# Norm tails of the GLU and the output projection: sums and products by column parts, and Newton steps on GpSimd

## The chip, the cores and the metric

The kernel runs on one core of a Trainium2 chip. The metric is the device time of one execution in microseconds (us), smaller is better. Five engines have queues of their own, each worked off in order: TensorE (PE; its weight loads are listed as PEld), VectorE (DVE), ScalarE (ACT), GpSimd (POOL) and SyncE (SP), which here issues most DMAs. Matmul results lie in PSUM, everything else on the chip in SBUF.

## What is computed

One inference step of a decoder trunk of two layers, for a prompt of 1024 tokens and 64 sample tokens (8 sequences of 8), model width D = 1024, in float32. Of the reference, the two places that matter here:

```python
def rmsnorm(x, g):
    y = xf * lax.rsqrt(jnp.mean(xf * xf, axis=-1, keepdims=True) + NORM_EPS)
    return (y * g)

def s5_mixer(...):                     # layer 0; ends with a gated linear unit (GLU)
    ...
    gl = z @ w_glu
    out = gl[..., :D_MODEL] * jax.nn.sigmoid(gl[..., D_MODEL:])

def trunk(...):
    # layer 0
    x = x + rmsnorm(a_out, p['a_post_g'][i])                 # a_out of s5_mixer
    # layer 1
    x = x + rmsnorm(o @ p['w_o'][j], p['b_post_g'][j])       # o of the attention
    # in both layers then
    f_out, buf = conv_ffn(rmsnorm(x, p['f_pre_g'][i]), ...)
    x = x + rmsnorm(f_out, p['f_post_g'][i])
```

Between the GLU or the output projection and the next feed-forward stage (conv_ffn, an up projection, a short convolution and a down projection) each token row therefore goes through two norms: the post-norm of what was just projected, and, after the residual is added, the pre-norm of the feed-forward stage.

## The kernel before

The tokens lie in nine tiles: eight of 128 prompt tokens (0 to 7) and one of the 64 sample tokens (8). A product in float32 is made of three matmuls over parts of high and low precision (`mm3`, L800 to L802), so operands are split into `hi` and `lo` (`split_evac`: a cast on ScalarE, L136, and a difference on VectorE, L137).

The **GLU** (`glu`) goes over the output columns in four passes `q` of 256 columns, and in each pass over the tiles in the order 0, 3, 1, 4, 2, 5, 6, 8, 7. Per tile and pass TensorE makes the two halves of `gl` in PSUM, ScalarE the sigmoid (L1022), VectorE the gated product into `ao[tt]` (L1023). In the last pass (q = 3) the row of a tile is complete, and its tail begins.

The **output projection** (`o_proj`) takes the tiles in the order 8, 0, 3, 1, 4, 2, 5, 6, 7. Columns 0 to 511 were made earlier and are loaded from `yod`; columns 512 to 1023 are made here, and copied out of PSUM by ScalarE (L1960). The tail follows per tile.

The **tail** of a tile has three parts. `tail_a`: the square sum of the row on ScalarE (L815), the product with the post-norm gain on VectorE (L829), the reciprocal root `r` of the mean square (`rstd_from`), and `r*y + xr` with the residual `xr` (L832), which is also stored. `tail_n`: the square sum of the result (L815 again), a second `rstd_from`, and the product with `r` and the pre-norm gain (L842). `tail_b`, some tiles later (`tail.lag`): TensorE transposes the row (L848) and `split_evac` splits it into the operand of the up projection. Tiles 3 to 5 also take part in pairs (`Combos.pair`: tile 0 with 3, 1 with 4, 2 with 5), where VectorE first makes four differences (L889 to L892).

`rstd_from` computes on 128x1 operands: L118 scales the sum, L119 makes a first guess from the bit pattern, and three Newton rounds follow, each L122 and L126, all on VectorE and each dependent on the one before it. A tile needs this twice.

The order of the instructions on each engine is not the order of the code: a scheduler places them by its own timing model, and so a change of one part shifts the neighbours too. Where the work of two tiles is ready, their Newton rounds are interleaved.

Of the kernel before, what the change touches and what calls it, by code (L numbers as in the profile page):

```python
# [10 lines left out]
F32 = mybir.dt.float32  # L11
# [62 lines left out]
def trunk_kernel(ctx, tc, I, O):  # L74
# [33 lines left out]
    def flat(t, n=512):  # L108
        return t[:, 0:n]

    def rstd_from(pool, ss, n, parts, tag, n_mean=D, bufs=None):

        kw = {"bufs": bufs} if bufs else {}
        v = pool.tile([P, n], F32, tag=tag + "v", name=nm("rv"), **kw)
        s = pool.tile([P, n], F32, tag=tag + "s", name=nm("rs"), **kw)
        r = pool.tile([P, n], F32, tag=tag + "r", name=nm("rr"), **kw)
        p = slice(0, parts)
        V.tensor_scalar(v[p], ss, -0.5 / n_mean, -0.5 * EPS, op0=ALU.mult, op1=ALU.add)  # L118
        V.tensor_scalar(r[p].bitcast(I32), v[p].bitcast(I32), -0.5, RSQ_MAGIC, op0=ALU.mult, op1=ALU.add)  # L119
        for _ in range(3):  # L120
            if n == 1:
                V.scalar_tensor_tensor(s[p], r[p], r[p], v[p], op0=ALU.mult, op1=ALU.mult)  # L122
            else:
                V.tensor_tensor(s[p], r[p], r[p], ALU.mult)
                V.tensor_tensor(s[p], s[p], v[p], ALU.mult)
            V.scalar_tensor_tensor(r[p], s[p], 1.5, r[p], op0=ALU.add, op1=ALU.mult)  # L126
        return r
# [684 lines left out]
    def square_sum(y, n):  # L812
        junk = slot("junk", dtype=BF16)
        ss = slot("ss")
        A.activation(junk[0:n], y, AF.Square, accum_out=ss[0:n])  # L815
        return ss[0:n]

    def rms_rstd(t, n):
        return rstd_from(pools["ph"], square_sum(t, n), 1, n, "n1", bufs=4)

    def tail_a(y, tt, post, xsrc, xdst, last=False):

        t0, n = tokens(tt)
        xr = slot("xr")
        nc.sync.dma_start(xr[0:n], xsrc(tt))
        halves = (slice(512, D), slice(0, 512)) if last else (slice(0, D),)
        ss = square_sum(y, n)
        for hs in halves:
            V.tensor_tensor(y[:, hs], y[:, hs], post[0:n, hs], ALU.mult)  # L829
        r = rstd_from(pools["ph"], ss, 1, n, "n1", bufs=4)  # L830
        for hs in halves:
            V.scalar_tensor_tensor(y[:, hs], y[:, hs], r[0:n], xr[0:n, hs], op0=ALU.mult, op1=ALU.add)  # L832
            nc.sync.dma_start(xdst(tt)[:, hs], y[:, hs])

    def tail_n(y, tt, gain=None):

        n = tokens(tt)[1]
        r = rms_rstd(y, n)
        if gain is None:
            A.mul(y, y, r[0:n])  # L840
        else:
            V.scalar_tensor_tensor(y, y, r[0:n], gain[0:n], op0=ALU.mult, op1=ALU.mult)  # L842
# [55 lines left out]
    class Tail:  # L898
# [2 lines left out]

        def __init__(self):
            self.n, self.q, self.combos, self.gain, self.lag = [], [], None, None, 2

        def add(self, y, tt, *a):
            tail_a(y, tt, *a)
# [86 lines left out]
    def glu(ws):  # L993
# [10 lines left out]
        for q in range(4):  # L1004
            if q:
                ws = glu_units(q)
            qs_ = slice(q * 256, (q + 1) * 256)
            for tt in ORDER_U:
                n = tokens(tt)[1]
                if q == 0:  # L1010
                    ao[tt] = slot("acc")
                    if tt == ORDER_U[4]:
                        tail_b(zt, NTT)
                        xsx = sample_pair()
                ps = tok_mm(tt, ws, None if n == P else xsx)
                if n < P:
                    g = slot("gr")[0:n]
                    fold_sample(g, ps)
                else:
                    g = ps  # L1020
                sg = slot("gr")
                A.activation(sg[0:n, 0:256], g[:, 256:512], AF.Sigmoid)  # L1022
                V.tensor_tensor(ao[tt][0:n, qs_], g[:, 0:256], sg[0:n, 0:256], ALU.mult)  # L1023
                if q == 3:
                    if tt == 0:
                        tail.combos = Combos()
                    y = ao[tt][0:n, 0:D]
                    tail.add(y, tt, post, x_in, x_scr(x1d))
            if q == 0:
                conv_params(0)  # L1030
                lam_column(cpool)
# [307 lines left out]

    def ffn_down(dn, i, xsrc, xdst, norm):  # L1340
        acc = {}
        post = [None]
        nch = len(dn.plan)

# [600 lines left out]
    def o_proj():  # L1945

        ws = half_units(I["w_o"][0], 1)
        post = row_bcast(I["b_post_g"][0])
        tail.gain, tail.lag = row_bcast(I["f_pre_g"][1]), 1
        conv_params(1)  # L1950
        xsx = sample_pair()
        for tt in ORDER_O:
            if tt == 0:
                tail.combos = Combos()
            t0, n = tokens(tt)
            y = slot("acc")
            nc.sync.dma_start(y[0:n, 0:512], yod[t0 : t0 + n])
            ps = tok_mm(tt, ws, xsx)
            if n == P:
                A.copy(y[:, 512:D], ps)  # L1960
            else:
                fold_sample(y[0:n, 512:D], ps)
            tail.add(y[0:n, 0:D], tt, post, x_scr(x2d), x_scr(x3d))
# [67 lines left out]
```

## Time and profile before

| | us |
|---|---|
| median of three runs (lowest, highest) | 2731.77 (2730.25, 2734.73) |
| profiled execution: its time, its span | 2735.75, 2734.0 |
| busy of the span: PE, DVE, ACT, POOL | 2519.4, 1957.0, 1260.9, 694.3 |

The profiled execution is 4 us above the median. The span goes from the first to the last instruction of that execution. Busy shares over the whole span mix stages with different limits; the stages that the change touches last from about 240 us (start of the GLU) to 490 us, and from about 1880 us to 1980 us (the output projection and its tails). In the profile's rows a duration is that of one record; records of neighbouring instructions on one engine can overlap by their start-up. "<-" names what ended an engine's wait.

### The profile page before, as it was taken

How to read it: one execution, taken by the hardware profiler on the slowest of the kernel's cores; microseconds unless marked ns; L12 is line 12 of the kernel's file. 1: busy time of each engine (PE TensorE's matmuls, PEld its weight loads, DVE VectorE, ACT ScalarE, POOL GpSimd, SP SyncE). 2: the span in 40 equal slices, each digit the busy share in tenths (PEclk: the TensorE clock that was granted, in tenths of full speed). 3: DMA queues.
4: the chain of work that ended last, by engine and by line, in shares of the span. 5: the costliest groups of instructions: out<-in, count | busy, mean ns of one | idle time of the engine just before them, and what ended most of it. 6: DMA issues, size and time to landing. Idle time of an engine off the chain costs nothing.

```text
span 2734.0 us, 39538 instructions
## 1 busy us (share of the span) xinstructions
PE 2519.4 (92%) x14362; PEld 2208.4 (81%) x14362; DVE 1957.0 (72%) x3719; ACT 1260.9 (46%) x2475; POOL 694.3 (25%) x943
## 2 busy tenths in 40 slices
PE   5778997999999989999999899999699999998996
PEld 3767886999999967778776788887599999996774
DVE  6994339677776789985222688866877767779998
ACT  5762225444444454344322677753444444454332
POOL 3220000111322375501201322200021222337661
PEclk9999998999999999999999999999899999999998
DMA  4343213222222233345645333325322222233324
GB/s 131 96 105 87 84 62 101 64 73 72 73 72 73 87 122 95 108 132 177 214 156 200 101 77 91 99 89 157 103 70 75 73 72 73 72 108 100 102 86 146
DMA packets 257702, 278.63 MB, mean 102 GB/s; under 512 B 41772, under 2 KB 205924, under 8 KB 257508
## 3 DMA queue, kind: packets, MB, share of 16 engines
q1 hardware_dynamic: 253188, 263.85, 31.3%
q0 software_dynamic: 3232, 10.29, 1.7%
q8 instruction: 114, 1.87, 0.3%
q10 hardware_dynamic: 1088, 1.97, 0.2%
q14 instruction: 80, 0.66, 0.1%
HBM read 187.82 MB, written 68.58 MB: 94 GB/s over the span
## 4 chain that ended last, share of the span: by engine, by line
PE 38%; DVE 9%; DMA 3%; ACT 3%; issue 2%; POOL 1%; SPq 0%; DVEq 0%; POOLq 0%; ACTq 0%
PE mm L800 11%; PE mm L801 10%; PE mm L802 10%; DVE S L1846 1%; ACT S L1850 1%; PE mm L1373 1%; DVE acc L1384 1%; DVE S L1860 1%; PE mm L1874 1%; DMA gr<-gd 1%; PE tr L848 1%; DVE qx L1789 1%; DMA raw<-in_w_down_dram 1%; DMA raw<-in_w_v_dram 1%; POOL xr L1265 0%
## 5 line engine op out<-in xcount | busy, mean ns | idle before, releaser
L800 PE MATMUL mm<-xT_hi,whi 128*128 128x320 f32 (+1 forms) x1408 | 459.4, 328 | 6.6 <-ACT xT_hi L136 3.4
L801 PE MATMUL mm<-xT_lo,whi 128*128 128x320 f32 (+1 forms) x1408 | 456.3, 324 | 0.1
L802 PE MATMUL mm<-xT_hi,wlo 128*128 128x384 f32 (+1 forms) x1408 | 454.7, 324 | 0.0
L1162 POOL COPY cvo<-acc 128x2 f32<-128x2 f32 x88 | 157.5, 1789 | 677.6 <-ACT acc L1145 677.6
L800 PEld LDWEIGHTS mm<-xT_hi,whi 128*128 128x128 f32 x1408 | 265.2, 189 | 15.6 <-DVE acc L1128 9.6
L137 DVE TENSOR_TENSOR wlo<-raw,whi 128x1024 fp32r<-128x1024 f32 x88 | 107.5, 1222 | 233.8 <-PE mm L801 227.3
L801 PEld LDWEIGHTS mm<-xT_lo,whi 128*128 128x128 f32 x1408 | 266.0, 189 | 0.9 <-DVE xT_lo L137 0.9
L802 PEld LDWEIGHTS mm<-xT_hi,wlo 128*128 128x128 f32 x1408 | 265.7, 189 | 0.2
L1159 DVE SCALAR_TENSOR_TENSOR acc<-acc,cpar,acc 128x1104 f32<-128x1104 f32 x176 | 238.8, 1377 | 0.7 <-ACT acc L1157 0.5
L800 PE MATMUL mm<-whi,xT_hi 128*128 128x512 f32 x576 | 228.6, 401 | 4.2 <-ACT whi L783 4.2
L801 PE MATMUL mm<-wlo,xT_hi 128*128 128x512 f32 x576 | 228.1, 397 | 0.0
L802 PE MATMUL mm<-whi,xT_lo 128*128 128x512 f32 x576 | 227.4, 397 | 0.0
L136 ACT CAST whi<-raw 128x1024 fp32r<-128x1024 f32 x88 | 92.7, 1054 | 286.1 <-PE mm L802 261.3
L1384 DVE TENSOR_TENSOR acc<-mm,acc 128x512 f32<-128x512 f32 x279 | 183.7, 678 | 5.0 <-PE mm L802 4.5
L800 PE MATMUL mm<-acc,whi 128*128 128x384 f32 x528 | 179.8, 341 | 3.1 <-DVE acc L1119 2.8
L801 PE MATMUL mm<-acc,whi 128*128 128x384 f32 x528 | 179.9, 341 | 0.0
L802 PE MATMUL mm<-acc,wlo 128*128 128x384 f32 x528 | 179.7, 341 | 0.0
L800 PEld LDWEIGHTS mm<-whi,xT_hi 128*128 128x128 f32 x576 | 108.7, 189 | 33.5 <-ACT whi L783 4.4
L802 PEld LDWEIGHTS mm<-whi,xT_lo 128*128 128x128 f32 x576 | 108.2, 188 | 26.6 <-issue 0.9
L1157 ACT ACTIVATE acc<-acc,cpar 128x1104 f32<-128x1104 f32 x88 | 115.4, 1313 | 30.5 <-DVE acc L1128 19.9
L801 PEld LDWEIGHTS mm<-wlo,xT_hi 128*128 128x128 f32 x576 | 108.2, 188 | 25.8 <-issue 0.4
L1846 DVE CUSTOM_DVE_ANT_0 S<-mm,tb 128x512 f32<-128x512 f32 (+3 forms) x192 | 101.1, 551 | 27.5 <-PE mm L1844 24.2
(563 smaller groups left out, 6255.9 us busy)
## 6 DMA issues: line engine op xcount, KB each, us to landing
raw<-in_w_up_dram SPq DMA_DIRECT2D x88, 512.0 KB
gd<-acc SPq DMA_DIRECT2D x44, 552.0 KB
raw<-in_w_down_dram SPq DMA_DIRECT2D x44, 512.0 KB
gr<-gd SPq DMA_DIRECT2D x80, 256.0 KB
raw<-in_glu_w_dram SPq DMA_DIRECT2D x32, 256.0 KB
acc<-in_cache_k_dram SPq DMA_DIRECT2D x16, 512.0 KB
acc<-in_cache_v_dram SPq DMA_DIRECT2D x16, 512.0 KB
xj<-in_x_prompt_dram SPq DMA_DIRECT2D x8, 512.0 KB
```

Of the source, the lines that this page charges most:

```text
L136: A.copy(hi_ap, ps_ap)
L137: V.tensor_tensor(lo_ap, ps_ap, hi_ap.bitcast(F32), ALU.subtract)
L800: PE.matmul(out, lh, rh, start=start, stop=False, **kw)
L801: PE.matmul(out, lh, rl, start=False, stop=False, **kw)
L802: PE.matmul(out, ll, rh, start=False, stop=stop, **kw)
L848: PE.transpose(ps[:, c * n : (c + 1) * n], y[:, c * P : (c + 1) * P], ident[0:n, 0:n])
L1157: A.activation(hc, hb[:, 2 : 2 + TG], AF.Identity, bias=cp[:, ft, 3:4], scale=cp[:, ft, 2:3])
L1159: V.scalar_tensor_tensor(hc, hb[:, tap : tap + TG], cp[:, ft, tap : tap + 1], hc, op0=ALU.mult, op1=ALU.add)
L1162: GP.tensor_copy(co[:, 0:2], hb[:, SEQ : SEQ + 2])
L1373: PE.matmul(pa[h], lt, wt[:, h * 512 : (h + 1) * 512], start=st and j == 0, stop=sp and j == len(seq) - 1)
L1384: V.tensor_tensor(a, ps, a, ALU.add)
L1846: V.tensor_tensor_reduce(S_[j][:, k0 : k0 + w], ps[:, 0:w], H["tb"][:, b0 : b0 + w], 0.125, -3e38, ALU.add, ALU.max, mx[:, j, c : c + 1])
```

## The change

1. *By parts.* A new function `part` takes the square sum and the post-norm product of some columns as soon as they exist: in the GLU 256 columns after each of the passes 0 to 2, in the output projection columns 0 to 511 after their load. ScalarE squares the part, GpSimd adds the scaled sum to a small buffer `pre` of the tile (one operation for the first part, two for a later one), VectorE multiplies the part by the gain. The last part is left to `tail_a`, whose first step of `rstd_from` now joins its sum with `pre`.
2. *Aside.* For tiles 0 to 5 the three Newton rounds of both norms, six operations each, are issued on GpSimd. This holds in the GLU and in the output projection, not in the down projections (`ffn_down`).

```diff
-    def rstd_from(pool, ss, n, parts, tag, n_mean=D, bufs=None):
+    def rstd_from(pool, ss, n, parts, tag, n_mean=D, bufs=None, pre=None, aside=False):
...
-        V.tensor_scalar(v[p], ss, -0.5 / n_mean, -0.5 * EPS, op0=ALU.mult, op1=ALU.add)
+        if pre is None:
+            V.tensor_scalar(v[p], ss, -0.5 / n_mean, -0.5 * EPS, op0=ALU.mult, op1=ALU.add)
+        else:
+            V.scalar_tensor_tensor(v[p], ss, -0.5 / n_mean, pre, op0=ALU.mult, op1=ALU.add)
         V.tensor_scalar(r[p].bitcast(I32), v[p].bitcast(I32), -0.5, RSQ_MAGIC, op0=ALU.mult, op1=ALU.add)
         for _ in range(3):
+            if aside:
+                GP.tensor_scalar(s[p], r[p], r[p], v[p], op0=ALU.mult, op1=ALU.mult)
+                GP.tensor_scalar(r[p], s[p], 1.5, r[p], op0=ALU.add, op1=ALU.mult)
+                continue
...
+    def aside(tt):
+        return tail.aside and tt < 6
+
+    def part(y, tt, post, c0, c1):
+        n = tokens(tt)[1]
+        ss = square_sum(y[:, c0:c1], n)
+        if c0:
+            p = sums[tt][0]
+            GP.tensor_scalar(ss, ss, -0.5 / D, None, op0=ALU.mult)
+            GP.tensor_tensor(p, ss, p, ALU.add)
+        else:
+            p = pools["ph"].tile([P, 1], F32, tag=f"pre{tt}", name=nm("pre"), bufs=1)[0:n]
+            GP.tensor_scalar(p, ss, -0.5 / D, -0.5 * EPS, op0=ALU.mult, op1=ALU.add)
+        V.tensor_tensor(y[:, c0:c1], y[:, c0:c1], post[0:n, c0:c1], ALU.mult)
+        sums[tt] = p, c1
...
     def tail_a(y, tt, post, xsrc, xdst, last=False):
-        ss = square_sum(y, n)
-        for hs in halves:
-            V.tensor_tensor(y[:, hs], y[:, hs], post[0:n, hs], ALU.mult)
-        r = rstd_from(pools["ph"], ss, 1, n, "n1", bufs=4)
+        pre, c = sums.pop(tt, (None, 0))
+        ss = square_sum(y[:, c:], n)
+        if c:
+            V.tensor_tensor(y[:, c:], y[:, c:], post[0:n, c:], ALU.mult)
+        else:
+            for hs in halves:
+                V.tensor_tensor(y[:, hs], y[:, hs], post[0:n, hs], ALU.mult)
+        r = rstd_from(pools["ph"], ss, 1, n, "n1", bufs=4, pre=pre, aside=aside(tt))
...
     def tail_n(y, tt, gain=None):
-        r = rms_rstd(y, n)
+        r = rstd_from(pools["ph"], square_sum(y, n), 1, n, "n1", bufs=4, aside=aside(tt))
...
     def glu(ws):
-                if q == 3:
+                if q < 3:
+                    part(ao[tt][0:n, 0:D], tt, post, 256 * q, 256 * q + 256)
+                else:
...
     def ffn_down(dn, i, xsrc, xdst, norm):
+        tail.aside = False
...
     def o_proj():
-        tail.gain, tail.lag = row_bcast(I["f_pre_g"][1]), 1
+        tail.gain, tail.lag, tail.aside = row_bcast(I["f_pre_g"][1]), 1, True
...
             nc.sync.dma_start(y[0:n, 0:512], yod[t0 : t0 + n])
+            part(y[0:n, 0:D], tt, post, 0, 512)
```

Lines of the changed kernel that answer to the old ones: L120 and L123 are the old L118 and L119; L122 is the new first step that joins `pre`; L130 and L134 are the Newton steps left on VectorE (old L122, L126), L126 and L127 those on GpSimd; L838, L839 and L842 are the GpSimd operations on `pre`, L843 the product of a part and L855 that of the last part (old L829); L145 the split (old L137), L861 and L871 the old L832 and L842, L877 the transposes (old L848), L918 to L921 the old L889 to L892, L1053 the old L1023.

In all, VectorE gets 3594 instead of 3702 rows in its queue and GpSimd 198 more: 72 Newton steps and 45 operations on `pre` in the GLU, 72 and 9 in the output projection. ScalarE gets 36 more squares.

VectorE's queue in the GLU's last pass, before. The names end in two running numbers; `rr` is the root, `rs` the inner value of a round, `rv` the scaled sum, `acc` a tile's row, `xr` the residual, `tr` transposed columns in PSUM.

```order
L122 SCALAR_TENSOR_TENSOR rs_590_3552<-rr_591_3553,rv_589_3551 128x1
L829 TENSOR_TENSOR acc_428_2494<-acc_428_2494,acc_417_2403 128x1024
L118 TENSOR_SCALAR rv_597_3597<-ss_596_3594 128x1
L126 SCALAR_TENSOR_TENSOR rr_586_3537<-rs_585_3536,rr_586_3537 128x1
L126 SCALAR_TENSOR_TENSOR rr_591_3553<-rs_590_3552,rr_591_3553 128x1
L119 TENSOR_SCALAR rr_599_3599<-rv_597_3597 128x1
L832 SCALAR_TENSOR_TENSOR acc_425_2465<-acc_425_2465,rr_586_3537,xr_581_3529 128x1024
L842 SCALAR_TENSOR_TENSOR acc_422_2436<-acc_422_2436,rr_591_3553,acc_418_2405 128x1024
```

The same queue in the changed kernel, where it holds the same kind of work:

```order
L123 TENSOR_SCALAR rr_677_3837<-rv_675_3835 128x1
L123 TENSOR_SCALAR rr_682_3853<-rv_680_3851 128x1
L921 TENSOR_TENSOR gr_686_3866<-acc_419_2407,gr_684_3864 128x512
L1053 TENSOR_TENSOR acc_452_2599<-mm_692_3912,gr_693_3937 128x256
L855 TENSOR_TENSOR acc_452_2599<-acc_452_2599,acc_417_2403 128x256
L122 SCALAR_TENSOR_TENSOR rv_697_3946<-ss_696_3943,pre_457_2631 128x1
L123 TENSOR_SCALAR rr_699_3948<-rv_697_3946 128x1
L145 TENSOR_TENSOR xT_lo_76<-tr_687_3871,xT_hi_75 128x4x128
L861 SCALAR_TENSOR_TENSOR acc_443_2547<-acc_443_2547,rr_677_3837,xr_672_3829 128x1024
L145 TENSOR_TENSOR xT_lo_76<-tr_688_3878,xT_hi_75 128x4x128
L871 SCALAR_TENSOR_TENSOR acc_437_2512<-acc_437_2512,rr_682_3853,acc_418_2405 128x1024
```

The Newton rounds of tiles 0 to 5 are gone from the queue, the product is one of 256 columns, and between L123, which starts a norm, and L861 or L871, which uses it, stand a combination, a gated product, a part product and one or two splits.

VectorE's queue in the output projection, before:

```order
L126 SCALAR_TENSOR_TENSOR rr_3275_18262<-rs_3274_18261,rr_3275_18262 128x1
L126 SCALAR_TENSOR_TENSOR rr_3290_18338<-rs_3289_18337,rr_3290_18338 128x1
L126 SCALAR_TENSOR_TENSOR rr_3280_18278<-rs_3279_18277,rr_3280_18278 128x1
L832 SCALAR_TENSOR_TENSOR acc_3268_18226<-acc_3268_18226,rr_3275_18262,xr_3270_18254 128x1024
L122 SCALAR_TENSOR_TENSOR rs_3289_18337<-rr_3290_18338,rv_3288_18336 128x1
L842 SCALAR_TENSOR_TENSOR acc_3246_18115<-acc_3246_18115,rr_3280_18278,acc_3171_17766 128x1024
L126 SCALAR_TENSOR_TENSOR rr_3290_18338<-rs_3289_18337,rr_3290_18338 128x1
L118 TENSOR_SCALAR rv_3293_18352<-ss_3292_18350 128x1
L889 TENSOR_TENSOR gr_3296_18364<-acc_3246_18115,acc_3231_18039 128x512
```

And in the changed kernel:

```order
L122 SCALAR_TENSOR_TENSOR rv_3354_18458<-ss_3353_18455,pre_3349_18423 128x1
L123 TENSOR_SCALAR rr_3356_18460<-rv_3354_18458 128x1
L120 TENSOR_SCALAR rv_3359_18474<-ss_3358_18472 128x1
L123 TENSOR_SCALAR rr_3361_18476<-rv_3359_18474 128x1
L843 TENSOR_TENSOR acc_3364_18500<-acc_3364_18500,acc_3233_17926 128x512
L855 TENSOR_TENSOR acc_3364_18500<-acc_3364_18500,acc_3233_17926 128x512
L122 SCALAR_TENSOR_TENSOR rv_3372_18540<-ss_3371_18537,pre_3367_18505 128x1
L123 TENSOR_SCALAR rr_3374_18542<-rv_3372_18540 128x1
L861 SCALAR_TENSOR_TENSOR acc_3346_18418<-acc_3346_18418,rr_3356_18460,xr_3351_18452 128x1024
L871 SCALAR_TENSOR_TENSOR acc_3321_18301<-acc_3321_18301,rr_3361_18476,acc_3234_17928 128x1024
L861 SCALAR_TENSOR_TENSOR acc_3364_18500<-acc_3364_18500,rr_3374_18542,xr_3369_18534 128x1024
```

Three norms (`rr_3356`, `rr_3361`, `rr_3374`) are started by L123 within this piece, and their three users follow in a row. What stands for them in GpSimd's queue, where there was no such work before:

```order
L842 TENSOR_SCALAR pre_3349_18423<-ss_3348_18421 128x1
L126 TENSOR_SCALAR rs_3355_18459<-rr_3356_18460,rv_3354_18458 128x1
L127 TENSOR_SCALAR rr_3356_18460<-rs_3355_18459,rr_3356_18460 128x1
L126 TENSOR_SCALAR rs_3360_18475<-rr_3361_18476,rv_3359_18474 128x1
L842 TENSOR_SCALAR pre_3367_18505<-ss_3366_18503 128x1
L126 TENSOR_SCALAR rs_3355_18459<-rr_3356_18460,rv_3354_18458 128x1
L127 TENSOR_SCALAR rr_3361_18476<-rs_3360_18475,rr_3361_18476 128x1
```

The chains of two norms are interleaved, and a `pre` operation of the next tile, which waits for ScalarE's square, stands between their steps.

More of the change, by code (lines that the diff above doesn't have):

```diff
@@ L814, in square_sum @@
         ss = slot("ss")
-        A.activation(junk[0:n], y, AF.Square, accum_out=ss[0:n])
+        A.activation(junk[0:n, 0 : y.shape[1]], y, AF.Square, accum_out=ss[0:n])
         return ss[0:n]
-    def rms_rstd(t, n):
-        return rstd_from(pools["ph"], square_sum(t, n), 1, n, "n1", bufs=4)
+    def aside(tt):
+        return tail.aside and tt < 6
+    sums = {}
+    def part(y, tt, post, c0, c1):
[10 more added lines that the diff above has]
+        sums[tt] = p, c1
     def tail_a(y, tt, post, xsrc, xdst, last=False):
@@ L903, in __init__ @@
             self.n, self.q, self.combos, self.gain, self.lag = [], [], None, None, 2
+            self.aside = True
         def add(self, y, tt, *a):
```

## The prediction

> **What bounds the kernel now.** I read the page first (busy shares, the chain that ended last), then the table by stretch at the two places that the diff touches, then what TensorE waits for there, then single instructions.
>
> ```profile
> PE 2519.4 (92%) x14362; PEld 2208.4 (81%) x14362; DVE 1957.0 (72%) x3719; ACT 1260.9 (46%) x2475; POOL 694.3 (25%) x943
> PE 38%; DVE 9%; DMA 3%; ACT 3%; issue 2%; POOL 1%; SPq 0%; DVEq 0%; POOLq 0%; ACTq 0%
> ```
>
> TensorE is 92% busy and leads the chain with 38%, against 9% for VectorE. Over the whole span VectorE's work is cheap; it counts only where TensorE stands still. The GLU's tails run from 430 us (below: start to end in us, busy us of PE, PEld, DVE, ACT, POOL, the granted clock, DMA share, GB/s), those of the output projection from 1920.
>
> ```profile
> 240.00:300.00 60.00, 60.00 (x287) 47.79 (x285) 19.12 (x48) 15.26 (x26) 0.00 (x0) 1.00 0.34 91
> 430.00:440.00 10.00, 7.16 (x40) 5.44 (x39) 8.65 (x27) 4.40 (x10) 0.00 (x0) 1.00 0.13 49
> 440.00:450.00 10.00, 3.15 (x13) 2.21 (x12) 9.66 (x23) 5.79 (x13) 0.00 (x0) 0.52 0.41 138
> 450.00:460.00 10.00, 6.72 (x23) 5.76 (x24) 9.95 (x35) 4.48 (x9) 0.00 (x0) 0.50 0.09 20
> 460.00:470.00 10.00, 8.54 (x51) 7.21 (x50) 10.00 (x24) 6.17 (x13) 1.58 (x4) 0.95 0.12 43
> 470.00:480.00 10.00, 8.10 (x42) 7.32 (x42) 9.75 (x24) 4.96 (x7) 0.00 (x0) 0.83 0.41 123
> 480.00:490.00 10.00, 7.37 (x42) 7.09 (x41) 6.29 (x11) 3.07 (x4) 0.00 (x0) 0.91 0.36 105
> ```
> ```profile
> 1920.00:1930.00 10.00, 0.21 (x1) 0.24 (x2) 8.86 (x31) 5.16 (x10) 0.00 (x0) 0.59 0.17 56
> 1930.00:1940.00 10.00, 4.56 (x20) 3.75 (x19) 9.23 (x27) 6.35 (x14) 0.00 (x0) 0.50 0.59 207
> 1940.00:1950.00 10.00, 6.80 (x28) 5.57 (x28) 10.00 (x36) 4.40 (x9) 0.23 (x2) 0.71 0.13 52
> 1950.00:1960.00 10.00, 8.09 (x48) 7.43 (x48) 9.50 (x24) 6.64 (x13) 1.06 (x2) 1.00 0.49 160
> 1960.00:1970.00 10.00, 8.43 (x42) 7.95 (x43) 9.32 (x18) 3.26 (x4) 0.00 (x0) 0.83 0.18 52
> ```
>
> From 430 to 490 TensorE is idle for 2.84+6.85+3.28+1.46+1.90+2.63 = 19.0 us, and between 440 and 460 its clock is halved besides; from 1920 to 1970 it is idle for 21.9 us. VectorE is full (8.65 to 10 of 10) until 480 and until 1970: there it is the bound. In the GLU's earlier passes (first row) it is busy for only 19.12 of 60 us. What TensorE's transposes (L848) waited for, first in 430 to 490, then in 1900 to 1980:
>
> ```profile
> PE tr L848 <- DVE rr L119: 4.3, 1, 4.3
> PE tr L848 <- DVE gr L889: 11.8, 2, 10.3
> ```
>
> In the GLU the wait is for the busy VectorE in general; in the output projection one wait of 10.3 us is for the first pair's combination (L889), so for a latency: products, two norms and a gain of two tiles in sequence.
>
> **What the change frees on VectorE.** Single instructions, first a norm whose steps run nearly alone, then steps between other work (start, duration):
>
> ```profile
> 395.72 0.42 DVE L1023 TENSOR_TENSOR acc<-mm,gr 128x256 f32<-128x256 f32 x1
> 396.06 0.14 DVE L119 TENSOR_SCALAR rr<-rv 128x1 int32<-128x1 int32 x1
> 396.24 0.22 DVE L122 SCALAR_TENSOR_TENSOR rs<-rr,rv 128x1 f32<-128x1 f32 x1
> 396.49 0.16 DVE L126 SCALAR_TENSOR_TENSOR rr<-rs,rr 128x1 f32<-128x1 f32 x1
> 396.69 0.22 DVE L122 SCALAR_TENSOR_TENSOR rs<-rr,rv 128x1 f32<-128x1 f32 x1
> 397.36 1.23 DVE L829 TENSOR_TENSOR acc<-acc,acc 128x1024 f32<-128x1024 f32 x1 [0.26 <-ACT gr L815]
> 398.50 0.21 DVE L122 SCALAR_TENSOR_TENSOR rs<-rr,rv 128x1 f32<-128x1 f32 x1
> ```
> ```profile
> 464.92 0.15 DVE L126 SCALAR_TENSOR_TENSOR rr<-rs,rr 128x1 f32<-128x1 f32 x1
> 464.99 0.20 DVE L122 SCALAR_TENSOR_TENSOR rs<-rr,rv 64x1 f32<-64x1 f32 x1
> 465.12 1.21 DVE L137 TENSOR_TENSOR wlo<-xr,whi 128x1024 fp32r<-128x1024 f32 x1
> ```
>
> Records of neighbours overlap, so what an instruction takes from the engine is the distance to the next start: 0.07 us for L126 (464.92 to 464.99) and 0.13 for L122 among other work; 0.20 and 0.25 where each waits for the one before it (396.24, 396.49, 396.69). A norm's three rounds cost 3 × 0.20 = 0.6 us interleaved or 3 × 0.45 = 1.35 alone. Twelve norms move at each place: 7.2 us at least, 16 at most. I take 7.2, since where VectorE is full another instruction fills the gap.
>
> The post-norm product L829 takes 1.14 us (397.36 to 398.50). Of the 256-column L1023 it is 0.34 (395.72 to 396.06). Nine GLU tiles save 9 × (1.14 − 0.34) = 7.2 us at the end. The 27 earlier parts cost 27 × 0.34 = 9.2 us in passes 0 to 2, where the row 240:300 leaves 41 of 60 us free on VectorE and 45 on ScalarE for the 27 added squares, and GpSimd is at 0.00 for the 45 operations on `pre`: nothing. If that cover failed, L843 would hold the next PSUM product behind it by at most 0.34 us per tile and pass.
>
> In the output projection the product is only cut in two. By the same two numbers 768 columns take 0.80 us, so 0.34 − 0.27 = 0.07 of an instruction is fixed, and nine more of them cost 0.6 us while VectorE is full. The first half's square leaves before the second half's matmul is done, but costs ScalarE a second accumulator read; ScalarE is at 3 to 7 of 10 there: nothing. No DMA is added, and the loads that trade places on SP's queue do so where DMA is under 0.6 of its share: nothing.
>
> Freed: GLU 7.2 + 7.2 = 14.4 us, output projection 7.2 − 0.6 = 6.6, together 21. Each microsecond counts fully, since VectorE is the bound at both places and TensorE's idle 19 and 21.9 us leave room for it.
>
> **What it adds: waits for GpSimd.** The trace has no such step on GpSimd. The nearest rows, L1162's tile view (min/median/max in ns) and two dependent operations:
>
> ```profile
> L1162 POOL COPY cvo<-acc x88: 176/1186/3625, 495.8 to 2440.7; 128x2 f32<-128x2 f32 x88
> ```
> ```profile
> 208.08 0.59 POOL L526 TENSOR_TENSOR dd<-ident,dT 16x128 f32<-16x128 f32 x1
> 208.75 0.44 POOL L527 TENSOR_TENSOR M<-M,dd 16x128 f32<-16x128 f32 x1
> ```
>
> A two-column copy takes 0.18 us at best, and a dependent one starts 0.08 after its predecessor's end (208.67 to 208.75): 6 × 0.26 = 1.56 us for a chain that nothing disturbs. The same copy took 3.62 us beside this:
>
> ```profile
> 574.81 3.62 POOL L1162 COPY cvo<-acc 128x2 f32<-128x2 f32 x1 [16.36 <-ACT acc L1145]
> 574.81 1.22 DVE L137 TENSOR_TENSOR wlo<-xr,whi 128x1024 fp32r<-128x1024 f32 x1
> 575.95 1.30 DVE L1170 TENSOR_TENSOR acc<-acc,acc 128x1104 f32<-128x1104 f32 x1
> 577.17 1.22 DVE L137 TENSOR_TENSOR wlo<-xr,whi 128x1024 fp32r<-128x1024 f32 x1
> 578.30 0.56 DVE L1122 TENSOR_TENSOR acc<-mm,acc 128x384 f32<-128x384 f32 x1
> ```
>
> It began with a row of VectorE products of two SBUF operands and ended 0.13 us after the first one with a PSUM operand began. So while L843, L855, L861, L871 or L918 to L920 run, a Newton step may get nowhere. This limits itself: once VectorE's queue stands at L861 or L871 waiting for the norm, nothing disturbs GpSimd and the rest of the chain takes at most 1.56 us. Over 24 chains the added wait is thus 0 to 37 us.
>
> Which value, by the order of the changed kernel: in the GLU a transposed split or a product from PSUM (L145, L1053) stands between a norm's start L123 and its L861 or L871 for most tiles; I take 0.5 us a chain, 6 us. In the output projection the queue reads L123, L843, L855, L122, L123, L861: two SBUF products, then the wait, with three chains and a `pre` step interleaved on GpSimd; L122 itself must wait for that `pre`, and ScalarE's squares, on four buffers, for the `pre` that frees one. I take 2 us for each of four groups of chains, 8 us. Everything behind L861 waits with it: the next products and the splits that TensorE's transposes need.
>
> **Sum.** GLU −14.4 + 6 = −8.4; output projection −6.6 + 8 = +1.4; together −7 us. On the profiled execution (span 2734.0, its time 2735.75) this gives 2728.7; that execution stood 4.0 over the median 2731.77, so on the median's scale it is **2724.7**. Ends: −21 with every wait hidden, +16 with every chain waited for in full. A change below 0.2% (5.5 us) can't be told from none.
>
> **Rivals.** *All covered* (0.12): VectorE always has other work; −21, 2711. The GLU's order speaks for it, the output projection's 10.3 us latency wait against.
>
> *Even* (0.20): waits of 21/24 = 0.88 us a chain eat what is freed: 2732. For it: a wait of 1.56 us at a little over half of the chains is enough.
>
> *The port* (0.26, slower): GpSimd's steps hold VectorE up as well, so that moved time isn't freed.
>
> ```profile
> 992.28 1.76 POOL L1265 TENSOR_TENSOR xr<-raw,xr 128x512 f32<-128x512 f32 x1
> 992.80 2.00 DVE L137 TENSOR_TENSOR xT_hi<-gr,xT_lo 128x256 fp32r<-128x256 f32 x2
> L137 DVE TENSOR_TENSOR xT_lo<-tr,xT_hi 128x256 fp32r<-128x256 f32 x2 | 0.8, 416 | 0.2 <-ACT xT_hi L136 0.2
> L832 DVE SCALAR_TENSOR_TENSOR acc<-acc,rr,xr 128x1024 f32<-128x1024 f32 x8 | 10.2, 1280 | 0.0
> L842 DVE SCALAR_TENSOR_TENSOR acc<-acc,rr,acc 128x1024 f32<-128x1024 f32 x8 | 10.2, 1278 | 0.0
> L889 DVE TENSOR_TENSOR gr<-acc,acc 128x512 f32<-128x512 f32 x3 | 2.0, 681 | 0.0
> ```
>
> (The rows from the third are groups of 390 to 500 us: busy us, mean ns of one, idle before.) Beside GpSimd's products (L1265 and what follows it) a 128x256 split of two SBUF operands took 1.00 us instead of the 0.416 with one in PSUM. The two places get 144 Newton and 9 `pre` steps of 0.18 us, 27 us; the two-SBUF lines L832, L842, L889 and L890 to L892 make 10.2 + 10.2 + 4 × 2.0 = 28 us, about half of the 54 that VectorE works from 430 to 490, so 14 of the 27 hold it up: −7 + 14 = +7, 2739; with all of it +20, 2752. It decides from 7 us on. Against it: at 574.81 VectorE kept its 1.22 us, and GpSimd paid.
>
> The Trainium skill ("SBUF — State Buffer", Who interferes with whom) states this as a lock: a VectorE instruction with two SBUF inputs and a GpSimd instruction that reads SBUF exclude each other, and whoever issues first blocks the other fully. Both rows agree, 3.62 us lost by GpSimd and 1.00 against 0.416 by VectorE; by the rule taken in both directions the port rival's time is the result, by the 574.81 row alone the forecast's. The skill ("GPSIMD Engine Reference", section 3.1 on elementwise work) also has GpSimd about 2× slower than VectorE; no run here shows a Newton step on it, and by that, as an estimate, a lone chain of 1.35 us would become 2.7 instead of 1.56 and the full wait 65 us instead of 37.
>
> **Chances.** Forecast 0.42 (own range 2718 to 2730), covered 0.12, even 0.20, port 0.26. Faster by over 0.2%: covered 0.12 and most of the forecast, 0.34. Within: 0.08 of the forecast, 0.16 of even, 0.02 of the port. Slower: the rest of even and port, 0.28. The range 2711 to 2743 reaches from the covered case into the port's; about a tenth lies beyond each end.
>
> **What would show it.** Right: 72 Newton steps on GpSimd at each place, near 0.2 us each, with a few of 1 to 3 us beside L861 and L871; the stretch 430 to 490 full of matmuls some 8 us earlier; 1920 to 1970 about unchanged, with waits of VectorE for GpSimd where L119's or L889's waits were; L1053 in passes 0 to 2 at its old pace with TensorE at 10 of 10. Wrong: L861, L871 and L918 to L921 longer than their old 1.28 and 0.68 us (the port); VectorE idle for over 21 us before L861 and L871 (even or slower); TensorE losing time before 390, which I priced at nothing.

## The result, and the profile after

The changed kernel takes 2740.07 us (median of 9 runs, 2735.79 to 2746.93) beside 2734.73 for the kernel before. The ratio is 1.0026, with a 95% interval from 1.0013 to 1.0038: slower by 4 to 10 us, where 2724.7, 7 us faster than the 2731.77 of the earlier three runs, was forecast. The profiled execution of the change is one of its shortest (2735.91, span 2733.8), so stages are compared and not spans.

Two stages hold what the diff touches. The GLU's goes from the first gated product to the first copy to `cvo` in the up projection (L1023 to L1162, after the change L1053 to L1194), the output projection's from its first copy out of PSUM (L1960, now L1994) to the same copy of the second layer. Rows of single lines give both (min/median/max in ns, then the first and the last start in us), first of before:

```profile
L1023 DVE TENSOR_TENSOR acc<-mm,gr x32: 406/425/425, 248.7 to 450.7; 128x256 f32<-128x256 f32 x32
L1960 ACT COPY acc<-mm x8: 567/589/603, 1878.4 to 1932.7; 128x512 f32<-128x512 f32 x8
L1162 POOL COPY cvo<-acc x44: 186/1186/3624, 1979.5 to 2440.7; 128x2 f32<-128x2 f32 x44
```

The first L1162 of all starts at 495.8, as a row of the prediction has it. After the change:

```profile
L1053 DVE TENSOR_TENSOR acc<-mm,gr x32: 405/425/426, 247.1 to 447.3; 128x256 f32<-128x256 f32 x32
L1194 POOL COPY cvo<-acc x88: 184/1235/3623, 488.5 to 2438.4; 128x2 f32<-128x2 f32 x88
L1994 ACT COPY acc<-mm x8: 564/590/606, 1866.0 to 1927.2; 128x512 f32<-128x512 f32 x8
L1194 POOL COPY cvo<-acc x44: 184/1218/3623, 1975.4 to 2438.4; 128x2 f32<-128x2 f32 x44
```

The GLU's stage went from 495.8 − 248.7 = 247.1 to 241.4 us, a gain of 5.7; the output projection's from 101.1 to 109.4, a loss of 8.3. The table by stretch shows the same (columns as in the prediction):

```profile
430.00:440.00 10.00, 5.11 (x26) 3.71 (x24) 7.80 (x19) 3.93 (x8) 5.64 (x12) 0.95 0.21 67
440.00:450.00 10.00, 5.34 (x23) 4.23 (x24) 9.23 (x34) 5.57 (x16) 0.00 (x0) 0.50 0.30 105
450.00:460.00 10.00, 8.48 (x39) 6.82 (x38) 10.00 (x22) 5.75 (x12) 2.15 (x2) 0.70 0.12 26
...
480.00:490.00 10.00, 8.65 (x56) 8.65 (x57) 3.30 (x5) 3.69 (x7) 0.82 (x2) 1.00 0.18 52
```
```profile
1906.00:1916.00 10.00, 3.42 (x20) 2.27 (x18) 8.06 (x19) 7.23 (x20) 2.90 (x6) 0.88 0.18 65
1916.00:1926.00 10.00, 1.72 (x8) 1.75 (x9) 6.51 (x10) 1.73 (x3) 6.95 (x17) 0.50 0.48 164
1926.00:1936.00 10.00, 5.29 (x25) 3.96 (x24) 9.28 (x27) 7.85 (x21) 4.74 (x15) 0.67 0.30 99
```

In the GLU TensorE is busier from 440 on (3.15, 6.72 and 7.37 in these stretches before). In the output projection TensorE is idle for 29.6 us of the stage instead of 24.1, and VectorE, which was at 8.86 to 10 of 10, falls to 6.51: it waits. A lower clock of TensorE is not the reason: over the two stages the granted clock was 0.96 and 0.88, against 0.94 and 0.86 before. What VectorE waited for, in 385 to 490 us and then in 1866 to 1986 (us in total, times, longest):

```profile
DVE acc L871 <- POOL rr L127: 4.7, 4, 1.7
DVE acc L861 <- POOL rr L127: 3.3, 4, 1.4
```
```profile
DVE acc L861 <- POOL rr L127: 7.4, 5, 2.0
DVE acc L871 <- POOL rr L127: 2.8, 4, 1.0
DVE rv L122 <- POOL pre L842: 1.0, 2, 0.5
```

That is 8.0 us for GpSimd in the GLU and 11.2 in the output projection, in 19 waits. TensorE's longest wait there, for a pair's difference, grew from 10.3 to 14.6 us. Its record, before and after:

```profile
1929.79 1.09 PE L848 MATMUL tr<-ident,gr 128*128 128x128 f32 x4 [10.32 <-DVE gr L889]
```
```profile
1924.28 1.09 PE L877 MATMUL tr<-ident,gr 128*128 128x128 f32 x4 [14.60 <-DVE gr L918]
```

The differences that it waits for start at 1928.97 and 1923.45, which is the second of three such in either stage (the first at 1907.03 and 1897.56): it is the pair of tiles 1 and 4, not the first pair, as the prediction had it. Counted from the stage's first copy it starts 50.6 us in before, 57.5 in the change.

A chain that nothing disturbs, a disturbed stretch with VectorE's instructions beside it (x2: two records in one row), and all 144 steps together:

```profile
1868.46 0.34 POOL L126 TENSOR_SCALAR rs<-rr,rv 128x1 f32<-128x1 f32 x1 [1.64 <-DVE rr L134]
1868.91 0.27 POOL L127 TENSOR_SCALAR rr<-rs,rr 128x1 f32<-128x1 f32 x1
1869.28 0.34 POOL L126 TENSOR_SCALAR rs<-rr,rv 128x1 f32<-128x1 f32 x1
...
1870.52 0.26 POOL L127 TENSOR_SCALAR rr<-rs,rr 128x1 f32<-128x1 f32 x1
```
```profile
1886.36 1.71 POOL L126 TENSOR_SCALAR rs<-rr,rv 128x1 f32<-128x1 f32 x2
1888.05 0.50 POOL L127 TENSOR_SCALAR rr<-rs,rr 128x1 f32<-128x1 f32 x2
1888.65 1.19 POOL L126 TENSOR_SCALAR rs<-rr,rv 128x1 f32<-128x1 f32 x1
```
```profile
1886.41 1.28 DVE L861 SCALAR_TENSOR_TENSOR acc<-acc,rr,xr 128x1024 f32<-128x1024 f32 x1 [1.63 <-POOL rr L127]
1888.34 1.28 DVE L871 SCALAR_TENSOR_TENSOR acc<-acc,rr,acc 128x1024 f32<-128x1024 f32 x1 [0.65 <-POOL rr L127]
```
```profile
L126 POOL TENSOR_SCALAR rs<-rr,rv 128x1 f32<-128x1 f32 x72 | 37.5, 526 | 28.0 <-DVE rr L123 21.9 <-DVE rr L134 1.6 <-DVE rv L120 1.5
L127 POOL TENSOR_SCALAR rr<-rs,rr 128x1 f32<-128x1 f32 x72 | 24.9, 352 | 3.6
```

Undisturbed, a chain of six takes from 1868.46 to 1870.78, 2.32 us, with 0.1 us between steps. An L126 that runs beside L861 or L871 takes more than 1 us instead of 0.34, while L861 and L871 keep their 1.28 us.

### The profile page after: what moved, and what is told of

The parts are those of the page before. It is cut to its first block, busy times and chain, and to the rows that moved or that the text cites. A ratio compares the mean times of both kernels' runs of the same rounds, so it can differ in the third digit from the quotient of the medians.

```text
span 2733.8 us, 39722 instructions
## 1 busy us (share of the span) xinstructions
PE 2523.4 (92%) x14362; PEld 2211.2 (81%) x14362; DVE 1946.0 (71%) x3611; ACT 1269.2 (46%) x2547; POOL 777.2 (28%) x1141
## 4 chain that ended last, share of the span: by engine, by line
PE 65%; DVE 16%; DMA 5%; ACT 5%; POOL 5%; issue 4%; SPq 1%; DVEq 0%; POOLq 0%; ACTq 0%
PE mm L808 18%; PE mm L809 18%; PE mm L810 18%; PE mm L1406 2%; DVE acc L1417 2%; DVE S L1879 1%; DVE xT_lo L145 1%; POOL rs L126 1%; DMA gr<-gd 1%; DMA raw<-in_w_up_dram 1%; DMA raw<-in_w_down_dram 1%; POOL xr L1297 1%; ACT S L1883 1%; PE mm L1907 1%; POOL rr L127 1%
## 5 line engine op out<-in xcount | busy, mean ns | idle before, releaser
L1194 POOL COPY cvo<-acc 128x2 f32<-128x2 f32 x88 | 159.7, 1814 | 682.8 <-ACT acc L1177 682.8
L145 DVE TENSOR_TENSOR wlo<-raw,whi 128x1024 fp32r<-128x1024 f32 x88 | 107.5, 1222 | 231.1 <-PE mm L809 227.8
```

What stands on the lines that cost most here:

```text
L145: V.tensor_tensor(lo_ap, ps_ap, hi_ap.bitcast(F32), ALU.subtract)
L1194: GP.tensor_copy(co[:, 0:2], hb[:, SEQ : SEQ + 2])
```

## The experiments

All stages below are read from the same two pairs of rows of one profiled execution of each kernel; the first execution of the change and its repetition (e10) differ by 0.0 and 0.9 us in them, and kernels whose code is the same in a stage by up to 1.6 us in the GLU (before and e4) and 1.9 in the projection (before, e3, e7, e11, e12). Smaller differences say nothing. "Ratio" is time over the kernel before, with its 95% interval; a microsecond is 0.037%.

| kernel | time, us | ratio | GLU stage | output projection stage |
|---|---|---|---|---|
| before | 2734.7 | 1 | 247.1 | 101.1 |
| the change | 2740.1 | 1.0026 (1.0013 to 1.0038) | 241.4 | 109.4 |
| e10 the change again | 2740.9 | 1.0027 (1.0016 to 1.0038) | 241.4 | 108.5 |
| e1 parts, no Newton steps aside | 2726.0 | 0.9970 (0.9958 to 0.9982) | 237.4 | 100.4 |
| e2 aside, no parts | 2743.1 | 1.0026 (1.0014 to 1.0038) | 250.2 | 108.0 |
| e3 the change in the GLU alone | 2732.8 | 0.9994 (0.9985 to 1.0003) | 241.8 | 102.1 |
| e4 the change in the output projection alone | 2742.7 | 1.0029 (1.0018 to 1.0040) | 245.5 | 107.8 |
| e5 parts, idle steps on GpSimd | 2732.3 | 0.9999 (0.9989 to 1.0008) | 237.6 | 106.2 |
| e6 the change with two rounds aside | 2727.6 | 0.9973 (0.9961 to 0.9985) | 236.0 | 102.8 |
| e7 parts in the GLU alone | 2726.1 | 0.9975 (0.9965 to 0.9985) | 237.4 | 101.1 |
| e8 parts, four tiles aside in the projection | 2730.7 | 0.9989 (0.9980 to 0.9998) | 237.5 | 106.6 |
| e16 as e8, but tiles 0, 2, 3, 5 | 2728.3 | 0.9981 (0.9970 to 0.9991) | 237.5 | 102.8 |
| e17 as e8, but tiles 2, 5 | 2725.5 | 0.9969 (0.9959 to 0.9980) | 237.4 | 101.4 |
| e9 the change, no rounds for six tiles | 2723.9 | 0.9970 (0.9960 to 0.9980) | 237.7 | 101.7 |
| e11 only the sums by parts, in the GLU | 2719.8 | 0.9952 (0.9939 to 0.9964) | 239.9 | 101.7 |
| e12 only the products by parts, in the GLU | 2712.9 | 0.9927 (0.9915 to 0.9939) | 236.7 | 100.2 |
| e13 parts, 144 idle steps more on VectorE | 2730.5 | 0.9985 (0.9975 to 0.9995) | 239.1 | 105.4 |
| e14 before, no rounds for six tiles | 2724.0 | 0.9960 (0.9947 to 0.9974) | 238.2 | 99.7 |
| e15 before, 144 idle steps more on VectorE | 2729.2 | 0.9984 (0.9973 to 0.9995) | 247.3 | 103.4 |

**One half, one place at a time (e1 to e4).** The edits, each alone, against the change:

```diff
 def aside(tt):                                   # e1
-    return tail.aside and tt < 6
+    return False
...
-                if q < 3:                        # e2, e4
-                    part(ao[tt][0:n, 0:D], tt, post, 256 * q, 256 * q + 256)
-                else:
+                if q == 3:
...
-            part(y[0:n, 0:D], tt, post, 0, 512)  # e2, e3; and tail.aside = False
                                                  # in the output projection (e3), in the GLU (e4)
```

> The whole change without its second half: products and sums by parts, all Newton steps on VectorE. Waiting theory (what lost the time is VectorE's wait for GpSimd's Newton chains, 11.2 us in the output projection and 8.0 in the GLU in the trace of the change): GLU gains about 7 us (nine products cut from 1.14 to 0.34), output projection +0 to +1, so about 6 us under before, near 2729, and no wait of VectorE for L127. Rival, the parts themselves cost (36 more squares, 63 operations on GpSimd, the earlier passes): 2735 or above. Rival, the loss lies outside the two places (clock phases later on): no different from the change, about 2740.

> The second half alone: Newton steps of tiles 0 to 5 on GpSimd at both places, products and sums whole as before. Waiting theory: each place frees 7.2 us of VectorE and waits 8 (GLU) to 11 us (output projection) for GpSimd, so GLU +1, output projection +4 to +8: 2740 to 2744 against 2735. Rival, parts are what costs: 2730 or below.

> The change in the GLU alone, the output projection as before. Waiting theory: the GLU place ends about 6 to 7 us earlier, as in the trace of the change, nothing is lost later: about 2728 to 2729 against 2735. Rival (the loss lies outside the two places, or the gain of the GLU is given back later): 2735 or above.

> The change in the output projection alone, the GLU as before. Waiting theory: from the first copy L1960 to the first L1162 of the second layer 8 us more than the 101 before, in all about 2743 against 2735. Rival (the loss lies elsewhere): 2735.

Parts alone are faster by 0.3%, and their gain in the GLU is 9.7 us where 7 were expected (they add 54 operations on GpSimd, not 63). Aside alone is slower by 0.26%. By stages, aside costs 3 to 4 us in the GLU (250.2 against 247.1, and 241.4 against 237.4) and 7 to 9 in the output projection (108.0 against 101.1, 109.4 against 100.4); parts gain 9 to 10 in the GLU and nothing clear of the spread in the projection. e4 puts the projection's loss where the waiting theory has it. e3 gained its 5 us in the stage, as forecast within 2 us, but its median came out only 0.9 under before (the interval allows 4): a miss. The two stages of the change sum to +2.6 us, under the lower end of what was measured (+4 to +10); where the remaining few microseconds lie can't be told from single executions, whose untouched stages differ by up to 4.5 us between the two executions of the change and by 5 to 10 from one kernel to another.

**Does GpSimd hold VectorE up, or only make it wait? (e5)** All Newton steps stay on VectorE, and GpSimd gets 144 steps whose results nobody reads:

```diff
             if aside:
-                GP.tensor_scalar(s[p], r[p], r[p], v[p], op0=ALU.mult, op1=ALU.mult)
-                GP.tensor_scalar(r[p], s[p], 1.5, r[p], op0=ALU.add, op1=ALU.mult)
-                continue
+                q2 = r2 if _ else v              # s2, r2: buffers of their own
+                GP.tensor_scalar(s2[p], q2[p], q2[p], v[p], op0=ALU.add, op1=ALU.add)
+                GP.tensor_scalar(r2[p], s2[p], 1.5, q2[p], op0=ALU.add, op1=ALU.add)
```

> Parts only, all Newton steps on VectorE in the same order as there, and beside them the same 144 small steps on GpSimd (additions in place of products, into buffers of their own): the result is not used, so VectorE never waits for a chain's end (but for `pre`, which queues among them, and for a buffer four norms later). Waiting theory (VectorE is slowed only by waiting for results of GpSimd): 2726 to 2729, as parts alone or a little more, VectorE's L861 and L871 start 1.19 us before their successors as before. Port theory (each GpSimd step, 0.3 us, holds VectorE's two-SBUF instructions up as well): 144 x 0.3 x a half = 21 us more, 2747.

The GLU's stage is 237.6 us against 237.4 with parts alone: 72 GpSimd steps beside VectorE cost it nothing. L864, this kernel's L861, keeps its duration there:

```profile
L864 DVE SCALAR_TENSOR_TENSOR acc<-acc,rr,xr 128x1024 f32<-128x1024 f32 x8 | 10.2, 1276 | 0.0
```

The port rival falls, though the time, 2732.3, is neither theory's. In the output projection the stage did grow by 5.8 us, the amount of VectorE's one kind of wait for GpSimd in 1855 to 1990:

```profile
DVE rv L122 <- POOL pre L845: 5.8, 2, 3.1
```

The sum `pre`, which is needed at once there, queued behind the idle steps; L864 keeps a mean of 1280 ns there too. So the amounts agree with queueing on GpSimd, and nothing shows a slower VectorE.

**Shorter chains (e6), fewer chains (e8).**

```diff
-        for _ in range(3):                       # e6
+        for _ in range(2 if aside else 3):
...
-        return tail.aside and tt < 6             # e8, and tail.aside = False in the GLU
+        return tail.aside and tt in (1, 2, 4, 5)
```

> The change with two Newton rounds instead of three on GpSimd (one round of the root is left out for tiles 0 to 5): chains of 4 steps. Waiting theory: each of the some 17 waits of VectorE for L127, 18 us in all, gets shorter by up to 2 x 0.42 us, so 10 to 14 us less waiting and 2728 to 2732 against 2740 of the change. Rival (the loss is not in the length of the chain, but in the order or in later stages): 2738 to 2740.

> Parts at both places, Newton steps on GpSimd only for tiles 1, 2, 4, 5 and only in the output projection: the first pair (tiles 0 and 3), for which TensorE waits 14.6 us at L918 in the change and 10.2 with parts alone, keeps its norms on VectorE. If the first pair's latency is what aside costs there, the stage from L1960 to L1162 comes back from 109 to 101 to 103 us and the time is 2727 to 2729; if every chain costs alike, 8 of 12 chains cost two thirds of 8 us, stage 106, time 2731 to 2732.

With two rounds the waits for L127 fall (here in 385 to 490, then in 1855 to 1990),

```profile
DVE acc L861 <- POOL rr L127: 3.1, 3, 1.3
DVE acc L871 <- POOL rr L127: 1.0, 2, 0.6
```
```profile
DVE acc L861 <- POOL rr L127: 3.3, 5, 1.3
DVE acc L871 <- POOL rr L127: 3.1, 5, 1.2
```

from 18.2 to 10.5 us, and the time falls by some 12 us, to 2727.6, just under the waiting theory's range. But the waits shrank by 7.7 us and not by 10 to 14, less than the time did, and the GLU's stage (236.0) ends as early as with parts alone although VectorE still waits 4.1 us in it: the wait is not the whole account. e8 gave its second number, 106.6 and 2730.7, but it rested on the wrong pair: the tiles 1 and 4, for which TensorE waits, were among the four whose norms stayed on GpSimd. e16 and e17 put that right, with e8's line naming other tiles:

```diff
-        return tail.aside and tt in (1, 2, 4, 5)
+        return tail.aside and tt in (0, 2, 3, 5)   # e16; (2, 5) in e17
```

> Parts at both places; in the output projection Newton steps on GpSimd for tiles 0, 2, 3, 5 only, so that the second pair (1 and 4), on whose difference L918 TensorE waits longest, keeps its norms on VectorE. If that pair's own chains are the cost: its L918 starts 50 to 51 us after the first L1994, as with parts alone (49.8), the stage is 101 to 103 us, 2726 to 2728. If any chain costs, since VectorE's queue stands still behind it: L918 at 53 to 55 us, as in e8 (54.9), stage 105 to 107, 2730 to 2732.

> As above with tiles 2 and 5 alone (the third pair), 4 of 12 chains, all behind the second pair's difference. If the second pair sets the stage: L918 of it at 50 us, stage 100 to 102, 2726. If every chain costs alike: a third of 8 us, stage 103, 2728 to 2729.

By the stage's length the second pair's chains look dearest. Against parts alone (100.4), tiles 2 and 5 aside cost 1.0 us, with 0 and 3 besides 2.4, with 1 and 4 besides 6.2, all six 8 to 9: tiles 1 and 4 add 5 to 7, the other pairs 1 to 3 each, little more than the spread. VectorE waited nearly as long for GpSimd in e16 (6.9 us, here in 1855 to 1990) as in e8 (6.8):

```profile
DVE acc L861 <- POOL rr L127: 4.1, 3, 1.6
DVE acc L871 <- POOL rr L127: 2.3, 4, 1.1
DVE rv L122 <- POOL pre L842: 0.5, 1, 0.5
```

But the mark that was set for it missed: the second pair's L918 starts at 54.7 us in e16 and 54.0 in e17, late as in e8 (54.9). Nor does the third pair's L918 tell them apart, first in e8 and then in e16 (whose stages start at 1868.4 and 1869.6):

```profile
1939.33 0.69 DVE L918 TENSOR_TENSOR gr<-acc,acc 128x512 f32<-128x512 f32 x1
```
```profile
1941.45 0.68 DVE L918 TENSOR_TENSOR gr<-acc,acc 128x512 f32<-128x512 f32 x1
```

That is 70.9 and 71.9 us into the stage, and by then the last chain on GpSimd is done and VectorE waits for it no more. What follows takes 35.7 us in e8 and 30.9 in e16. VectorE's queue stands in another order there: the last L861 starts 79.7 us into the stage in e8, behind several splits, and 75.8 in e16. So the difference between the two kernels arises behind the chains, and that the chains of tiles 1 and 4 themselves are the cost is not shown.

The change can be divided in the same way. The third difference, before and after:

```profile
1947.28 0.69 DVE L889 TENSOR_TENSOR gr<-acc,acc 128x512 f32<-128x512 f32 x1
```
```profile
1939.56 0.68 DVE L918 TENSOR_TENSOR gr<-acc,acc 128x512 f32<-128x512 f32 x1
```

It starts 68.9 us into the stage before and 73.6 in the change: 4.7 of the 8.3 us are lost by then, while VectorE waits for GpSimd. The other 3.6 (2.6 in e10) come behind it, where no chain is left and the order is another (last L861 at 81.4 us, before at 71.4). In e5, which waits only for `pre`, all of the loss lies before the third difference (74.2 us, against 68.2 in e1). That the order by itself costs these 3 us was not tested.

**What the freed time is worth (e9, e13 to e15).** e9 leaves the rounds out for tiles 0 to 5 (their roots stay the first guess), so that nothing waits for GpSimd's chains; e14 does so in the kernel before. e13 and e15 add 144 steps to VectorE that nobody reads, to parts and to the kernel before:

```diff
-        for _ in range(3):                       # e9, e14
+        for _ in range(0 if aside else 3):
...
+                V.scalar_tensor_tensor(s2[p], q2[p], q2[p], v[p], op0=ALU.add, op1=ALU.add)    # e13, e15
+                V.scalar_tensor_tensor(r2[p], s2[p], 1.5, q2[p], op0=ALU.add, op1=ALU.add)
```

> The change with no Newton rounds at all for tiles 0 to 5 in the two places (their roots stay at the first guess of L123): what VectorE's 144 steps are worth when they vanish and nothing waits for GpSimd. If each freed microsecond counts fully, as the prediction had it: against parts alone GLU stage 237.4 - 7.2 = 230 us, output projection 100.4 - 7.2 = 93 us, 2712 in all. Rival, the steps filled gaps in which VectorE would have stood anyway: stages 235 and 98 or more, 2720 or above.

> The change once more, beside the kernel above: 2737 to 2742; stages as in its first profile, GLU 241 us, output projection 109 us, with 8 and 11 us of VectorE waiting for GpSimd. If the loss were chance of the clock in later stages, the two stages would come out as before by more than 2 us.

> Parts at both places with all Newton steps on VectorE, and 144 more small steps of the same kind on VectorE (additions into buffers that nobody reads). If VectorE's time is the bound: 0.6 us a norm, stages 237.4 + 7.2 = 245 and 100.4 + 7.2 = 108 us, 2740 in all. If the stages' ends hang on other chains: 238 and 101, 2726 to 2728.

> The kernel before (product and sum whole) without the Newton rounds of tiles 0 to 5 at both places (their roots stay at the first guess). If VectorE's time is the bound: stages 247.1 - 7.2 = 240 and 101.1 - 7.2 = 94, 2719 in all. If it saturates (counts in the GLU until the parts' gain is reached): 240 and 100 to 102, 2726. If it never counts: 246 and 101, 2732.

> The kernel before with 144 more small steps on VectorE that nobody reads, 72 at each place. If VectorE's time is the bound: 254 and 108 us, 2748 in all. If not: 248 and 102, 2735.

Against e1, e9 changes the stages by +0.3 and +1.3 us, where −7.2 each would have come if each freed microsecond counted. The whole of 390 to 490 us, of e1 and then of e9:

```profile
390.00:490.00 100.00, 87.34 (x446) 74.87 (x446) 85.37 (x253) 44.29 (x96) 4.30 (x8) 0.93 0.32 105
```
```profile
390.00:490.00 100.00, 87.29 (x448) 75.06 (x448) 80.76 (x183) 46.27 (x100) 5.02 (x10) 0.93 0.31 101
```

VectorE works 4.6 us less and TensorE is as busy as before, 87.29 against 87.34: the freed time became idle time of VectorE. Over the stage itself, which starts 3.5 us earlier in e9, VectorE works 119.8 us instead of 127.1, and TensorE stands idle for 12.7 us in both. In e9's output projection it shows as waits for the split's first half, ScalarE's cast of the transposes (1855 to 1975 us; 1.1 in e1):

```profile
DVE xT_lo L145 <- ACT xT_hi L144: 6.0, 3, 3.6
```

In the kernel before, the same removal gains 8.9 us in the GLU (e14, 238.2) and 1.4 in the projection; adding steps costs 0.2 and 2.3 there (e15), and 1.7 and 5.0 on top of parts (e13). So in the GLU there are two levels, about 247 and about 238 us. Either remedy alone, parts or fewer Newton steps, reaches the lower one; both together do no better. In the projection work added lengthens the stage, and work taken away doesn't shorten it beyond the spread. What holds the GLU's lower level wasn't settled: the scheduler reorders the neighbours in each of these kernels, and no run here kept its order fixed.

**Which half of the parts (e7, e11, e12).** e7 is e1 without the cut in the output projection. e11 and e12 are e7 with one half each; in e12 the square sum is taken whole over a row whose first 768 columns are multiplied already, so the norm is of another row.

```diff
-            part(y[0:n, 0:D], tt, post, 0, 512)  # e7, e11, e12; aside(tt) returns False
...
-        V.tensor_tensor(y[:, c0:c1], y[:, c0:c1], post[0:n, c0:c1], ALU.mult)   # e11, in part
...
-        ss = square_sum(y[:, c0:c1], n)          # e12, in part; and no operations on pre
```

> Parts in the GLU only; the output projection and all Newton steps as before. If cutting the product in two in the output projection is worth nothing (stage 100.4 us with it, 101.1 and 102.1 without), this gives the time of parts alone, 2726. If the earlier first half shortens the first pair's latency, 2728 to 2729.

> Parts in the GLU only and of them only the sums: ScalarE squares by parts with GpSimd's `pre`, the product with the gain stays whole in the tail (1.14 us on VectorE). All Newton steps on VectorE. If the gain of the parts is VectorE's 9 x 0.8 = 7.2 us at the end, the GLU stage stays at 245 to 247 us, 2733 in all. If it is the shorter square (1.06 to 0.38 us in front of each norm), the stage goes to 238 to 241 and the time to 2727 to 2729.

> Parts in the GLU only and of them only the products: the square sum is taken whole in the last pass, over a row whose first 768 columns are multiplied already (so the norm is of another row). All Newton steps on VectorE. If the gain is VectorE's 7.2 us, the GLU stage is 238 to 240 us and the time 2726 to 2728, as with parts whole. If it is the shorter square, the stage is 244 to 247 and the time 2731 to 2734.

e7 takes the time of e1: cutting the product in the output projection is worth nothing. Sums alone take 7.2 us from the GLU's stage, products alone 10.4, both 9.7. They don't add either, which is the same lower level again. The times of e11, e12 and e15 are lower than these stages explain, by some 7, 10 and 7 us. In e11 the first layer's feed-forward stage, from its first `cvo` copy to its last sum of the down projection (L1384 before), takes 689.2 us instead of 696.6 (692.1 to 697.9 in the others); in e12 and e15 that of the second layer takes 724.4 and 724.0 instead of 732.7 (731.0 to 737.0 in the others). In the down projection of these three the instructions of every engine stand in another order than in the other kernels, in code that these edits don't touch; that the order is the cause was not tested by itself. e11 leaves nothing out of the computation and, at 2719.8, is faster than both kernels, though only half of its gain lies in the stage that it edits.

## Why the prediction was wrong

*What bounds the stages.* "Each microsecond counts fully, since VectorE is the bound" is the step that failed. A busy share of 9 to 10 in ten showed a full VectorE and not that the stage's end hung on the sum of its work. Of the 14.4 us priced for the GLU, 9.7 came with the parts, more than their 7.2, and the 7.2 of the Newton steps were worth nothing on top of them (stage +0.3, e9 against e1), though 8.9 without them (e14): the two gains don't add. In the output projection 6.6 us were priced and none came: parts gave 0.7 and the missing Newton steps −1.3, both within the 1.9 us by which stages of the same code differ there. The 10.3 us wait quoted there was the warning, though put down to the wrong pair: e9 takes 36 Newton rounds from VectorE, and the difference that TensorE waits for starts 49.9 us into the stage, as with parts alone (49.8).

*The chain on GpSimd.* 1.56 us was taken from the shortest copy of two columns (0.18) and one gap (0.08). Measured, a step with its gap takes 0.39 us, a chain 2.32 alone, and the 144 steps, disturbed or not, average 0.43 us without gaps. The waits were sized 6 and 8 us and measured 8.0 and 11.2, a third and two fifths more. That waits limit themselves held in the change: its longest was 2.0 us, less than a chain.

*The sum.* −8.4 and +1.4 us were forecast, −5.7 and +8.3 came. e9, the change without its chains, splits them, as far as two kernels of different order can. What was freed gave −9.4 us in the GLU, where −14.4 was forecast, and +0.6 in the projection, where −6.6 was; with the chains the stages are 3.7 and 7.7 us longer, where 6 and 8 were priced. So the freed time is the term that was wrong, by 5 and 7 us; the waits lasted longer than forecast, and the stages still lost no more by them than was priced. The sign set for *slower*, over 21 us of waiting, did not come either: 18.2 us in front of L861 and L871 were enough, because less was freed. With the freed Newton time at nothing and the waits as sized, the same sum would give +7 us, inside what was measured, but with −1.2 in the GLU, where −5.7 came: that agreement is partly chance.

*What held.* The earlier passes took the added products, squares and `pre` operations for nothing: TensorE stays at 10 of 10 until 430 us in the change (and in e1, 40.00 of 40 from 390 to 430). The starving of GpSimd beside two-SBUF instructions, seen at 574.81, is what the chains met. The cut in two of the projection's product is worth nothing that can be told (e7).

*The rivals.* The port's time, 2739, is the one that came (2740.1), but not by its mechanism: L861 and L871 kept their 1.28 us, and 144 idle steps on GpSimd left the GLU's stage as it was (e5). That the number agrees is chance. "Even" had the right mechanism, waits that eat what is freed, and the wrong balance, since less was freed than waited for. Of the Trainium skill's lock ("SBUF — State Buffer", Who interferes with whom) these runs show one direction for the small steps: GpSimd's steps of 0.34 us grew past 1 us, VectorE's L861 stayed at 1.28. The Trainium skill's factor of 2 for GpSimd ("GPSIMD Engine Reference", section 3.1) was nearer than my row: 2.32 against 1.35 us is 1.7.

*What stays open.* What holds the GLU at its lower level, how much of the projection's loss is order rather than waiting, and where the rest of the change's time lies beyond its two stages.

## What to carry to other kernels

A full engine is shown to be the bound only if taking work from it moves the end: before pricing freed time, ask what its queue would do next, and compare a kernel that simply leaves the work out with one that keeps it. Moving a short dependent chain to another engine trades issue time on one queue for a wait at the chain's user, so its full length on the new engine must be covered by work between start and use, above all on the path for which the next engine waits. A time that comes true is no proof of the mechanism that forecast it, as the port's shows. Making sums and products when their columns appear, in passes where VectorE, ScalarE and GpSimd have room, shortened the GLU's tail without any such wait.

## What the runs showed of the hardware that was not expected

Operations of one column on GpSimd take 0.34 us with two scalars read from SBUF and 0.27 with one and a constant, with 0.1 us between dependent ones, against 0.25 and 0.20 from start to start on VectorE. Between these steps and VectorE's products of 1.28 us only GpSimd paid: its steps grew past 1 us, and 144 of them added no time to the products. GpSimd's wider products, beside which the prediction's row at 992.80 shows a slower split, were not tested.
